# Down-projection prepared ahead, and four merge blocks beside the last head's close

## Chip, cores and metric

The kernel runs on one core of a Trainium2 chip. The metric is the device time of one execution in microseconds (us), the median of several runs. The core's engines are TensorE (PE in the profile, with its weight loads as PEld), VectorE (DVE), ScalarE (ACT), GpSimd (POOL) and SyncE (SP), whose queue here issues all DMAs. Each engine works through its own list in a fixed order.

## What is computed

One layer of a streaming encoder, for 1024 rows of a prompt and 8 x 16 rows of samples, 1152 rows of 1024 features in float32. Cut to what matters here:

```
# three mixers on slices of h @ w_in; B is a gated recurrence in 4 heads of 128
o_b = merge_heads(rms_norm_gated(o_b, hgrn_w, heads(bg, B_VAL_DIM)))
gates = sigmoid(gt.reshape(bsz, t, N_BRANCH, D_MODEL))
mix = gates[:, :, 0] * (o_a @ w_ba) + gates[:, :, 1] * (o_b @ w_bb) + gates[:, :, 2] * (o_c @ w_bc)
x = layer_norm(ALPHA * x + mix @ w_out, ln1_g, ln1_b)
up, new_ffn_conv = causal_dwconv(x @ w_up, buf_ffn, f_conv_w)     # 2 x 2816 columns
gate, val = split(up + f_conv_b, 2)
x = layer_norm(ALPHA * x + (silu(gate) * val) @ w_down, ln2_g, ln2_b)
```

## The kernel before

Rows of tokens are cut into three blocks of 384 (n = 0, 1, 2), features into tiles of 128. Each float32 operand is split in a high part and a rest, by a cast on ScalarE and a subtraction on VectorE, and a product is three matmuls: high by high, high by rest, rest by high. In the names, o, x1 and mix have parts with h and l, and whl, w8, wres and wd are weights with both parts.

A scheduler in the compiler orders each engine's list from the order of the program, the buffers and its own model of time. A pool gives each tag a ring of buffers; a new tile waits until the old one in its place is done with. `beside` puts a generator on a side list that `tick` advances between matmuls, so `yield 2` means "two ticks later". `drain` runs the side list out. `keep_in_program_order` holds an instruction at its place on its engine.

**The last head and the merge.** Heads of the mixers run as generators beside the projections' blocks. A head's last step, `finish_group` (L700), multiplies the head's output oT by its norm factor (L703; the factor comes from nine tiny VectorE operations named nwi, nwa, nwy), transposes it on PE (L148), multiplies it by the gate z2 (L709) and stores it to d_o. Then `load_o` (L1485) loads the four heads' outputs of a block of tokens and splits them into o (L1478, L1479); the last tile of four is called z. The merge multiplies o by the branch weights, 12 matmuls a block (24 blocks for branch 1: m = 0 to 7 for each n), and `branch_ev` (L1512) evicts each with a gate tile from d_g: one multiplication (L1517) and one addition into mix (L1518). Weights wb 0 to 3 lie in whl, 4 to 7 in wres (L1566, L1567). L1559 drains the side list, the last head among it, before the first block of branch 1. Then follow w_out (weights L1600) and the norm.

**Up-projection.** Column tiles come in 22 pairs of gate and value. From the third pair on, the token blocks 0 and 1 are done by a scheme of seven half-size products in place of eight, with sums of features (the four tiles ts) and of weights; block 2 is done plainly. `Pair.put` takes a product out of PSUM, `Pair.conv` does the convolution over three rows, which needs the two rows ahead of the block, and stores to d_gu.

**Down-projection.** It has 66 steps: for each half of the 22 feature tiles, for each token block n, for each tile k of the half. A step needs the weight rows wd[k] (loaded and split only for n = 0: L1957, L1958) and the features gd (two loads from d_gu, multiplied in L1962, split in L1965 and L1966). It makes 18 matmuls into six PSUM banks, for three row tiles by two halves of the columns; after eleven steps the six banks are added into yac (L2054). `residual` loads nine yac tiles and the norm's vectors gb (L1939) and turns them into the scaled residual (L1943, L1944). `prepare` (L2047) runs up to eight steps ahead. All of this is issued after the up-projection's last block and a drain.

Of the kernel before, what the change touches and what calls it, by code (L numbers as in the profile page):

```python
# [17 lines left out]
P = 128  # L18
# [53 lines left out]
def tile_encoder_step(ctx: ExitStack, tc: tile.TileContext, cst, x_prompt, x_sample, cache_k, cache_v, st_hgrn,  # L72
# [73 lines left out]
    def tr(out, in_):  # L146
        n = in_.shape[0]
        PE.transpose(out, in_, ident[:n, :n])  # L148
# [551 lines left out]

    def finish_group(oT, fac, wcol, z2, out):

        V.tensor_mul(u3(oT), u3(oT), bc(fac, 3))  # L703
# [688 lines left out]
    def b_finish(hd, n):  # L1392
        x, h = hd.g[n], hd.h

        so = small("rq2", [P, 3], 2)
        V.tensor_scalar(so, x.ss, 1.0 / P, 4 * RMS_EPS, ALU.mult, ALU.add)
        yield 1
        yield from finish_group(x.oT, rsqrt(cur[0], so, 3), vcol("hgw", 0), hd.z[n], d_o[1][h * P:(h + 1) * P, tok(n)])

# [33 lines left out]

    done = [0]

# [181 lines left out]

    oh, ol, _ = parts[1]
    mh = [[None] * NBLK for _ in range(KD)]
# [12 lines left out]
    for n in range(NBLK):  # L1632
        if n:
            beside(mix_split(n - 1))

        for i, m in enumerate((4, 5, 6, 7, 0, 1, 2, 3) if n == 2 else range(KD)):
            block(wb[m], oh, ol, n, branch_ev(1, m), kt=4)
            if n == 0 and i in (2, 5):
                load_in_turn(gb[:, i // 3], (ln_in_g, ln_in_b)[i // 3].partition_broadcast(P))
# [80 lines left out]
    class Pair:  # L1720
# [5 lines left out]
        def tail(self):  # L1726
            yield 5
# [94 lines left out]
    def x_sums():  # L1822
        for k in range(H):
            t = wfp_().bitcast(F32)
            t = t.rearrange("p a b c -> p (a b c)")[:, :4 * NW].rearrange("p (a w) -> p a w", w=NW)
            for a, (kk, n) in enumerate(((k, 0), (k, 1), (k + H, 0), (k + H, 1))):
                V.tensor_add(t[:, a], xh[kk][n].bitcast(F32), xl[kk][n].bitcast(F32))
                yield 1
# [5 lines left out]
            yield 1  # L1834
            hl = xs.tile([P, 2, 4, NW], F32R, name=f"ts{k}")
            S.copy(hl[:, 0], t)
# [42 lines left out]
    T1, T3, T4, T2 = ((lambda k, a=a: (ts[k][:, 0, a], ts[k][:, 1, a])) for a in range(4))  # L1879
    B11, B21, B22 = ((lambda k, k0=k0, n=n: (xh[k0 + k][n], xl[k0 + k][n])) for k0, n in ((0, 0), (H, 0), (H, 1)))  # L1880

# [9 lines left out]
    for i, pr in enumerate(rest):  # L1891
# [10 lines left out]
        p5 = product(pr.s12, 0, T1)  # L1902
        pr.put(0, 0, product(pr.a1, 1, B21), p1)
        pr.conv(0, 0)
        next(parts_[i + 1], None)
        V.tensor_add(u3, u2, product(pr.s34, 0, T3))
        V.tensor_add(u2, u2, p5)
        pr.put(1, 1, p5, u3)
        pr.put(0, 1, product(pr.s34, 1, B22), u2)
        pr.conv(0, 1)  # L1910
        gate_rest = lambda pr=pr: block(pr.a1, xh, xl, NBLK - 1, pr.ev(0))
        behind = lambda pr=pr: block(pr.a2, xh, xl, NBLK - 1, pr.ev(1))
        if i < len(rest) - 1:
            gate_rest()
            next(parts_[i + 1])
        pr.put(1, 0, product(pr.a2, 1, T4), u3)
        pr.conv(1, 0)
        pr.conv(1, 1)
    gate_rest()
    behind()  # L1920

    drain()
    xs_ctx.close()
    late.close()
    s0_ctx.close()
# [4 lines left out]
    yac = [yp.tile([P, D], F32, name=f"yac{j}") for j in range(NT)]  # L1930
    wd, gd = {}, {}
    late_w = lambda: dp.tile([P, 2, D], F32R, tag="wd", name=nm("wd"), bufs=12)

    def residual():
        gb = dp.tile([P, 2, D], F32, name="gb2")
        for i, src in enumerate((ln1_g[0], ln1_b[0])):
            load(gb[:, i], src.partition_broadcast(P))
        yield 6
        S.mul(gb, gb, ALPHA)  # L1939
        for j in range(NT):  # L1940
            load(yac[j], d_xn1[j * P:(j + 1) * P, :])
            yield 3
            V.tensor_mul(yac[j], yac[j], gb[:, 0])  # L1943
            V.tensor_add(yac[j], yac[j], gb[:, 1])  # L1944
            yield 3
        for t, src in enumerate((ln2_g, ln2_b)):
            load(gb[:, t], src[0].partition_broadcast(P))
        lnv.append(gb)

    lnv = []  # L1950

    def prep_step(half, n, k):
        if n == 0:
            raw = dp.tile([P, D], F32, tag="wdr", name=nm("wdr"), bufs=2)
            load(raw, w_down[0, k * P:(k + 1) * P, :])
            hl = wd[k] = late_w()
            S.copy(hl[:, 0], raw)  # L1957
            V.tensor_sub(hl[:, 1], raw, hl[:, 0].bitcast(F32))  # L1958
        raw = dp.tile([P, 2, NW], F32, tag="gr", name=nm("gr"), bufs=3)
        for half_ in range(2):  # L1960
            load(raw[:, half_], d_gu[half_][k][:, tok(n)])
        V.tensor_mul(raw[:, 0], raw[:, 0], raw[:, 1])  # L1962
        raw = raw[:, 0]
        g = gd[k, n] = dp.tile([P, 2, NW], F32R, tag="gd", name=nm("gd"), bufs=13)
        S.copy(g[:, 0], raw)  # L1965
        V.tensor_sub(g[:, 1], raw, g[:, 0].bitcast(F32))  # L1966

    def terms(ps, k, n, i, cs, first, stop):
        g, sl = gd[k, n], slice(i * P, (i + 1) * P)
        mm(ps, g[:, 0, sl], wd[k][:, 0, cs], start=first, stop=False)  # L1970
        mm(ps, g[:, 1, sl], wd[k][:, 0, cs], start=False, stop=False)
        mm(ps, g[:, 0, sl], wd[k][:, 1, cs], start=False, stop=stop)

# [28 lines left out]
    def last_ln(j):  # L2002
        y = yac[j]
        g2, b2 = lnv[0][:, 0], lnv[0][:, 1]
        if j == NT - 1:
# [19 lines left out]
        V.tensor_scalar(s[:, 2:3], s[:, 0:1], s[:, 1:2], -1.0 / D, ALU.add, ALU.mult)  # L2025
        squares = dp.tile([P, D], F32, tag="wdr", name=nm("wdr"), bufs=2)
        S.activation(squares, y, AF.Square, bias=s[:, 2:3], accum_out=s[:, 3:4])
# [14 lines left out]
    cols = [slice(hf * 512, (hf + 1) * 512) for hf in range(2)]  # L2042
    rows_of = [range(0, NFF // 2), range(NFF // 2, NFF)]
    steps = [(half, n, k) for half in range(2) for n in range(NBLK) for k in rows_of[half]]
    ahead = [0]

    def prepare(upto):  # L2047
# [4 lines left out]
    def put_sum(half, j, hf, ps):  # L2052
        if half == 0 or j == NT - 1:
            V.tensor_add(yac[j][:, cols[hf]], yac[j][:, cols[hf]], ps)  # L2054
# [65 lines left out]
```

## Time and profile before

| | us |
|---|---|
| median of 3 runs | 2266.27 (2265.26 to 2268.82) |
| the profiled execution | 2266.73 |
| its span in the trace | 2264.9 |
| TensorE busy | 2178.8 (96%) |
| VectorE busy | 1530.2 (68%) |
| ScalarE busy | 982.7 (43%) |

A row of a timeline has the start in us, the duration (of all merged instructions together), the engine, the line, the operation, output and inputs, the count, and in brackets how long the engine was idle before and what ended that. Matmuls overlap, so the rate is read from the starts of rows. The trace's clock of TensorE over the whole run was 0.985 of full.

### The profile page before, as it was taken

The page shows a single profiled execution, that of the slowest core. Times are in us where ns is not written, and L with a number is a line of the kernel's source. Part 1 is how long each engine was busy: PE and PEld are TensorE (multiplying, and loading weights), DVE is VectorE, ACT ScalarE, POOL GpSimd, SP SyncE. Part 2 cuts the span into 40 slices and gives each one's busy share as a digit, 9 for nine tenths or more (in the row PEclk, how much of TensorE's full clock was granted, in tenths as well). Part 3 has the DMA queues.
Part 4 walks back from the last instruction along what each step waited for, and adds up shares of the span by engine and source line. Part 5 has one row for each costly group of instructions (what it writes and reads, how often), then busy time and mean ns, then how long its engine had stood idle before and what let it go on. Part 6 is the DMA issues. An engine that isn't in the chain of part 4 may idle for free.

```text
span 2264.9 us, 35159 instructions
## 1 busy us (share of the span) xinstructions
PE 2178.8 (96%) x12759; PEld 2030.1 (90%) x12759; DVE 1530.2 (68%) x4246; ACT 982.7 (43%) x2309; POOL 1.3 (0%) x9
## 2 busy tenths in 40 slices
PE   7999999999999999999999899999999999689998
PEld 7998889999999999999989888899999999567886
DVE  7367556666765657767878786877777777674444
ACT  4356434344345346355433333544545445231234
POOL 0000000000000000000000000000000000000000
PEclk9999999999999999999999999999999999899999
DMA  5121231222222221312354541232323232674421
GB/s 139 44 76 56 86 102 48 74 73 65 69 78 57 76 60 52 94 42 64 119 157 137 164 151 75 70 102 94 102 97 108 92 97 76 224 233 128 155 98 56
DMA packets 261373, 220.30 MB, mean 97 GB/s; under 512 B 38810, under 2 KB 250688, under 8 KB 261184
## 3 DMA queue, kind: packets, MB, share of 16 engines
q1 hardware_dynamic: 261200, 218.06, 31.1%
q8 instruction: 100, 1.64, 0.3%
q14 instruction: 73, 0.60, 0.1%
HBM read 152.86 MB, written 66.06 MB: 97 GB/s over the span
## 4 chain that ended last, share of the span: by engine, by line
PE 85%; DVE 5%; DMA 5%; ACT 3%; issue 1%; SPq 1%; DVEq 0%; ACTq 0%
PE psg L108 72%; PE psp L108 5%; PE psch L108 4%; DMA gr<-d_gu 2%; PE psp L148 2%; PE psch L148 1%; PE psms L108 1%; PE psms L148 1%; DMA xp<-d_o 1%; SPq L111 1%; DVE gr L1962 0%; DVE yac L1944 0%; DVE gd L1966 0%; ACT L1223 0%; DVE yac L1943 0%
## 5 line engine op out<-in xcount | busy, mean ns | idle before, releaser
L108 PE MATMUL psg<-hh,whl 128*128 128x384 f32 x2976 | 809.0, 344 | 0.8 <-ACT qf L436 0.7
L108 PEld LDWEIGHTS psg<-hh,whl 128*128 128x128 f32 x2976 | 535.6, 188 | 15.4 <-issue 8.6
L108 PE MATMUL psg<-hl,whl 128*128 128x384 f32 x1488 | 508.5, 342 | 0.0
L108 PE MATMUL psg<-wd,gd 128*128 128x512 f32 x1188 | 277.0, 396 | 30.9 <-ACT gd L1965 11.2
L108 PEld LDWEIGHTS psg<-wd,gd 128*128 128x128 f32 x1188 | 227.1, 192 | 80.6 <-ACT gd L1965 11.4
L108 PEld LDWEIGHTS psg<-hl,whl 128*128 128x128 f32 x1488 | 280.1, 188 | 4.3 <-issue 2.6
L108 PE MATMUL psg<-x1h,w 128*128 128x384 f32 x672 | 182.0, 340 | 0.0
L108 PE MATMUL psg<-x1h,whl 128*128 128x384 f32 x640 | 172.7, 339 | 2.8 <-ACT whl L212 1.2
L108 PE MATMUL psg<-o,whl 128*128 128x384 f32 x720 | 142.8, 349 | 6.6 <-ACT o L1478 2.6
L108 PEld LDWEIGHTS psg<-o,whl 128*128 128x128 f32 x720 | 127.3, 194 | 9.8 <-ACT o L1478 3.2
L108 PEld LDWEIGHTS psg<-x1h,w 128*128 128x128 f32 x672 | 122.9, 188 | 1.0
L108 PEld LDWEIGHTS psg<-x1h,whl 128*128 128x128 f32 x640 | 116.9, 189 | 4.9 <-ACT whl L212 1.9
L108 PE MATMUL psg<-x1l,w 128*128 128x384 f32 x336 | 113.5, 338 | 0.0
L213 DVE TENSOR_TENSOR whl<-wraw,whl 128x1024 fp32r<-128x1024 f32 (+1 forms) x82 | 91.5, 1117 | 31.9 <-ACT whl L212 30.8
L108 PE MATMUL psg<-x1l,whl 128*128 128x384 f32 x320 | 108.2, 338 | 0.0
L108 PE MATMUL psg<-ts,w 128*128 128x384 f32 x576 | 105.8, 334 | 0.0
L108 PEld LDWEIGHTS psg<-ts,w 128*128 128x128 f32 x576 | 100.6, 188 | 0.0
L1962 DVE TENSOR_TENSOR gr<-gr 128x384 f32<-128x384 f32 x66 | 36.7, 557 | 92.7 <-DMA gr<-d_gu 92.2
L212 ACT CAST whl<-wraw 128x1024 fp32r<-128x1024 f32 (+1 forms) x82 | 79.0, 964 | 36.8 <-PE psg L108 34.4
L108 PE MATMUL psg<-wres,mixh 128*128 128x512 f32 x288 | 92.5, 395 | 0.0
L1965 ACT CAST gd<-gr 128x384 fp32r<-128x384 f32 x66 | 33.8, 512 | 129.5 <-PE psg L108 78.3
L1445 ACT ACTIVATE ga<-psg 128x384 f32<-128x384 f32 x72 | 35.4, 491 | 97.6 <-PE psg L108 80.0
(505 smaller groups left out, 3829.1 us busy)
## 6 DMA issues: line engine op xcount, KB each, us to landing
wraw<-in_w_in_dram SPq DMA_DIRECT2D x58, 512.0 KB
gr<-d_gu SPq DMA_DIRECT2D x132, 192.0 KB
d_g<-ga SPq DMA_DIRECT2D x72, 192.0 KB
wraw<-in_w_up_dram SPq DMA_DIRECT2D x24, 512.0 KB
wdr<-in_w_down_dram SPq DMA_DIRECT2D x22, 512.0 KB
wr<-in_w_up_dram SPq DMA_DIRECT2D x20, 512.0 KB
acc<-d_g SPq DMA_DIRECT2D x48, 192.0 KB
d_gu<-ga SPq DMA_DIRECT2D x44, 192.0 KB
```

What stands on the lines that cost most here:

```text
L108: PE.matmul(out, lhsT, rhs, start=start, stop=stop)
L111: nc.sync.dma_start(out=out, in_=in_)
L148: PE.transpose(out, in_, ident[:n, :n])
L212: S.copy(hl[:, 0, :kt, :cols], raw[:, :kt, :cols])
L213: V.tensor_sub(hl[:, 1, :kt, :cols], raw[:, :kt, :cols], hl[:, 0, :kt, :cols].bitcast(F32))
L1445: S.activation(g, ps, AF.Tanh, scale=0.5)
L1962: V.tensor_mul(raw[:, 0], raw[:, 0], raw[:, 1])
L1965: S.copy(g[:, 0], raw)
```

## The change

At the end of the mixers, the program no longer drains before branch 1: it ticks only until the last head is about to finish (`ended`), issues the weights and the first four blocks of the merge (m = 0 to 3, n = 0), and then drains. The last head's `finish_group` waits ten ticks, and its first transpose is held in its place.

In the up-projection, the roles of token blocks 0 and 1 in the scheme of seven are exchanged, so that block 0 of the value and of the gate are taken out and convolved together; an output chain (`tail`) waits ten ticks, not five. The tiles ts come from a ring of four.

The down-projection's first two weights, in the buffers wraw and whl, and the features of its first four steps, in one tile g4 in the ring of ts, are prepared ahead of the up-projection's last two blocks (`ending`). Steps 2 and 3 have their raw weights loaded there too. yac lies in the other three tiles of that ring, three rows of tokens in each, and `residual` is run once for each token block. Features have two buffers of raw data and twelve split ones (three and thirteen before), weights twelve in all as before, two of them whl. `put_sum` gets a higher priority with the scheduler.

```diff
-    def finish_group(oT, fac, wcol, z2, out):
+    def finish_group(oT, fac, wcol, z2, out, behind=False):
         V.tensor_mul(u3(oT), u3(oT), bc(fac, 3))
-        yield 2
+        yield 10 if behind else 2
         ps = psum("ms")
         for i in range(3):
-            tr(ps[:, i * P:(i + 1) * P], oT[:, i * P:(i + 1) * P])
+            t = PE.transpose(ps[:, i * P:(i + 1) * P], oT[:, i * P:(i + 1) * P], ident)
+            if behind and i == 0:
+                tc.keep_in_program_order(t)
...
-    drain()
+    while not ended[0]:
+        tick()
...
     whl_pair(2)
+
+    oh, ol, _ = parts[1]
+    for m in range(4):
+        block(wb[m], oh, ol, 0, branch_ev(1, m), kt=4)
+    drain()
...
-    for m in range(3):
+    for m in range(4, 7):
         gate_ahead[1, m, 0] = load_gate(1, m, 0)
...
+            if n == 0 and i < 4:
+                continue
             block(wb[m], oh, ol, n, branch_ev(1, m), kt=4)
...
-        pr.put(0, 0, product(pr.a1, 1, B21), p1)
-        pr.conv(0, 0)
+        pr.put(0, 1, product(pr.a1, 1, B21), p1)
...
-        pr.put(1, 1, p5, u3)
-        pr.put(0, 1, product(pr.s34, 1, B22), u2)
+        pr.put(1, 0, p5, u3)
+        pr.conv(1, 0)
+        pr.put(0, 0, product(pr.s34, 1, B22), u2)
+        pr.conv(0, 0)
         pr.conv(0, 1)
...
+    def prep_weights(k):
+        raw, hl = raw_w(), two_w()
+        load(raw, w_down[0, k * P:(k + 1) * P, :])
+        S.copy(hl[:, 0], raw)
+        V.tensor_sub(hl[:, 1], raw, hl[:, 0].bitcast(F32))
+        wd[k] = hl
+
+    def prep_features(n, k, raw, gh, gl):
+        for half in range(2):
+            load(raw[half], d_gu[half][k][:, tok(n)])
+        V.tensor_mul(raw[0], raw[0], raw[1])
+        S.copy(gh, raw[0])
+        V.tensor_sub(gl, raw[0], gh.bitcast(F32))
+        gd[k, n] = gh, gl
+
+    EARLY = 4
+    g4 = quarter_of_xs("g4")
+    for s in range(EARLY):
+        if s < 2:
+            prep_weights(s)
+        prep_features(0, s, [s0_piece("gr", F32) for _ in range(2)], g4[:, 0, s], g4[:, 1, s])
+    ahead[0] = EARLY
+    ending()
     drain()
...
+    for k in range(2, EARLY):
+        prep_weights(k)
...
     def put_sum(half, j, hf, ps):
-        if half == 0 or j == NT - 1:
-            V.tensor_add(yac[j][:, cols[hf]], yac[j][:, cols[hf]], ps)
-        else:
-            add_and_sum(j, hf, cols[hf], ps)
+        with tc.high_priority(60):
...
-            if (half, n) == (0, 0):
-                prepare(3)
-                beside(residual())
+            if half == 0:
+                beside(residual(n), 12 if n == 0 else 1)
...
-                    prepare(min(at + 8, 3 + 2 * at))
+                    prepare(at + 8 if at > 1 else at + 6 + at)
```

How this moves instructions on the engines is shown at three places. First PE, at the last head's close: psms is the transposed output of the last head, psg with whl or wres the blocks of branch 1. Before:

```order
L108 MATMUL psg_14526<-o_13770,whl_14385 128x384
L108 MATMUL psg_14526<-o_13769,whl_14385 128x384
L148 MATMUL psms_14348<-call,oT_14211 128x128 x3
L108 MATMUL psg_14601<-o_14463,whl_14439 128x384
L108 MATMUL psg_14601<-o_14464,whl_14439 128x384
```

and of the change:

```order
L108 MATMUL psg_14526<-o_13769,whl_14378 128x384
L108 MATMUL psg_14572<-o_14463,whl_14439 128x384
...
L108 MATMUL psg_14623<-o_14481,whl_14567 128x384
L707 MATMUL psms_14422<-call,oT_14211 128x128 x3
L108 MATMUL psg_14669<-o_14463,wres_14658 128x384
L108 MATMUL psg_14669<-o_14464,wres_14658 128x384
L108 MATMUL psg_14685<-o_14463,wres_14658 128x384
```

The transposes moved behind the four blocks (psg_14572 to psg_14623, 48 matmuls), and what comes next on PE needs wres.

On ScalarE, what casts wres stands behind the cast of the last head's z tile, in both programs. Of the change:

```order
L1572 CAST whl_14567<-wraw_14568 128x1024
L1483 CAST o_14557<-v_14555 128x384
L1483 CAST o_14563<-z_14561 128x384
L1572 CAST wres_14658<-wraw_14659 128x1024
L1572 CAST wres_14663<-wraw_14664 128x1024
```

Here nothing moved; PE's rows around it did.

Second VectorE at the same place, one piece of the difference: the rows with acc are evictions of the four blocks (psg_14572 and on), those with mix their additions, and oT is what the transposes wait for.

```order
+L1522 SCALAR_TENSOR_TENSOR acc_14619<-acc_14619,psg_14606 128x384
+L1523 TENSOR_TENSOR mix_12568<-mix_12568,acc_14602 128x384
 L327 SCALAR_TENSOR_TENSOR nwy_14318<-nwa_14315,nwi_14312 128x3
+L1523 TENSOR_TENSOR mix_12571<-mix_12571,acc_14619 128x384
 L324 TENSOR_TENSOR nwa_14320<-nwy_14318 128x3
+L1522 SCALAR_TENSOR_TENSOR acc_14636<-acc_14636,psg_14623 128x384
 L325 SCALAR_TENSOR_TENSOR nwa_14320<-nwa_14320,rq_3024_14297 128x3
+L1523 TENSOR_TENSOR mix_12574<-mix_12574,acc_14636 128x384
 L327 SCALAR_TENSOR_TENSOR nwy_14323<-nwa_14320,nwy_14318 128x3
```

All four blocks' evictions now stand inside the chain of small operations that leads to oT; before, they stood behind it.

Third the DMA queue of SP, where the up-projection ends. d_gu<-gv are its last feature stores, wdr and wraw raw down-projection weights, gr features, yac residual rows. Before:

```order
L111 DMA yac_21665<-d_xn_118 128x1024
L111 DMA d_gu_21_16097<-gv_21591 128x384
...
L111 DMA d_gu_21_16119<-gv_21631 128x384
L111 DMA wdr_21668<-in_w_down_dram 128x1024
L111 DMA gr_21673<-d_gu_0_16076 128x384
L111 DMA gr_21673<-d_gu_0_16098 128x384
```

and of the change:

```order
L111 DMA wraw_21694<-in_w_down_dram 128x1024
L111 DMA d_gu_20_16118<-gv_21423 128x384
L111 DMA wraw_21699<-in_w_down_dram 128x1024
...
L111 DMA d_gu_21_16119<-va_21492 128x384
...
L111 DMA d_gu_21_16119<-gv_21670 128x384
L111 DMA out_dram<-r_4256_21676 16x128
L111 DMA gr_21718<-d_gu_4_16080 128x384
L111 DMA gr_21718<-d_gu_4_16102 128x384
L111 DMA gr_21730<-d_gu_5_16081 128x384
```

The weights of steps 2 and 3 are now loaded about one pair earlier, those of steps 0 and 1 earlier still; behind the last store stand the features of step 4, and no residual rows stand ahead of it.

More of the change, by code (lines that the diff above doesn't have):

```diff
@@ L1396, in b_finish @@
         V.tensor_scalar(so, x.ss, 1.0 / P, 4 * RMS_EPS, ALU.mult, ALU.add)
+        last = (h, n) == (3, NBLK - 1)
         yield 1
-        yield from finish_group(x.oT, rsqrt(cur[0], so, 3), vcol("hgw", 0), hd.z[n], d_o[1][h * P:(h + 1) * P, tok(n)])
+        ended[0] = last
+        yield from finish_group(x.oT, rsqrt(cur[0], so, 3), vcol("hgw", 0), hd.z[n], d_o[1][h * P:(h + 1) * P, tok(n)],
+                                last)
     heads = []
@@ L1432, in b_group @@
         done[0] += 1
-    done = [0]
+    done, ended = [0], [False]
     GT = 4872
@@ L1616, in rows_h @@
         V.tensor_add(t, t, gb[:, 1])
-    oh, ol, _ = parts[1]
     mh = [[None] * NBLK for _ in range(KD)]
@@ L1636, in tile_encoder_step @@
         for i, m in enumerate((4, 5, 6, 7, 0, 1, 2, 3) if n == 2 else range(KD)):
+            if n == 0 and i < 4:
+                continue
             block(wb[m], oh, ol, n, branch_ev(1, m), kt=4)
-            if n == 0 and i in (2, 5):
-                load_in_turn(gb[:, i // 3], (ln_in_g, ln_in_b)[i // 3].partition_broadcast(P))
+            if n == 0 and i in (4, 6):
+                load_in_turn(gb[:, i // 2 - 2], (ln_in_g, ln_in_b)[i // 2 - 2].partition_broadcast(P))
             if n == 1 and i == 3:
@@ L1726, in tail @@
         def tail(self):
-            yield 5
+            yield 10
             ps1 = psum("ms")
@@ L1811, in tile_encoder_step @@
     xs = xs_ctx.enter_context(tc.tile_pool(name="xs", bufs=1, side="right", reuse_waits="tile"))
+    quarter_of_xs = lambda name: xs.tile([P, 2, 4, NW], F32R, tag="ts", name=nm(name), bufs=4)
     H = KD // 2
@@ L1825, in x_sums @@
             t = t.rearrange("p a b c -> p (a b c)")[:, :4 * NW].rearrange("p (a w) -> p a w", w=NW)
-            for a, (kk, n) in enumerate(((k, 0), (k, 1), (k + H, 0), (k + H, 1))):
+            for a, (kk, n) in enumerate(((k, 1), (k, 0), (k + H, 1), (k + H, 0))):
                 V.tensor_add(t[:, a], xh[kk][n].bitcast(F32), xl[kk][n].bitcast(F32))
@@ L1834, in x_sums @@
             yield 1
-            hl = xs.tile([P, 2, 4, NW], F32R, name=f"ts{k}")
+            hl = quarter_of_xs("ts")
             S.copy(hl[:, 0], t)
@@ L1879, in tile_encoder_step @@
     T1, T3, T4, T2 = ((lambda k, a=a: (ts[k][:, 0, a], ts[k][:, 1, a])) for a in range(4))
-    B11, B21, B22 = ((lambda k, k0=k0, n=n: (xh[k0 + k][n], xl[k0 + k][n])) for k0, n in ((0, 0), (H, 0), (H, 1)))
+    B11, B21, B22 = ((lambda k, k0=k0, n=n: (xh[k0 + k][n], xl[k0 + k][n])) for k0, n in ((0, 1), (H, 1), (H, 0)))
     beside(x_sums())
@@ L1914, in tile_encoder_step, with ending @@
             gate_rest()
-            next(parts_[i + 1])
-        pr.put(1, 0, product(pr.a2, 1, T4), u3)
-        pr.conv(1, 0)
+            next(parts_[i + 1], None)
+        pr.put(1, 1, product(pr.a2, 1, T4), u3)
         pr.conv(1, 1)
-    gate_rest()
-    behind()
+    def ending():
+        gate_rest()
+        behind()
+    raw_w = lambda: wp.tile([P, D], F32, tag="wraw", name=nm("wraw"), bufs=2)
+    two_w = turn(*2 * [lambda: wp.tile([P, 2, D], F32R, tag="whl", name=nm("whl"), bufs=2)],
+                 *10 * [lambda: dp.tile([P, 2, D], F32R, tag="wd", name=nm("wd"), bufs=10)])
@@ new lines, in tile_encoder_step @@
+    wd, gd = {}, {}
+    rows_of = [range(0, NFF // 2), range(NFF // 2, NFF)]
+    steps = [(half, n, k) for half in range(2) for n in range(NBLK) for k in rows_of[half]]
+    ahead = [0]
+    def prep_weights(k):
[11 more added lines that the diff above has]
+        gd[k, n] = gh, gl
@@ L1930, in tile_encoder_step @@
[L1930 to L1942, printed above, removed]
+    yac = []
@@ new lines, in tile_encoder_step, with residual @@
+    for n in range(NBLK):
+        y3 = quarter_of_xs("yac").bitcast(F32).rearrange("p a b c -> p (a b c)")
+        yac += [y3[:, i * D:(i + 1) * D] for i in range(3)]
+    for k in range(2, EARLY):
+        prep_weights(k)
+    gb = dp.tile([P, 2, D], F32, name="gb2")
+    def residual(n):
+        if n == 0:
+            for i, src in enumerate((ln1_g[0], ln1_b[0])):
+                load_in_turn(gb[:, i], src.partition_broadcast(P))
+            S.mul(gb, gb, ALPHA)
+            yield 2
+        for j in range(3 * n, 3 * n + 3):
+            load_in_turn(yac[j], d_xn1[j * P:(j + 1) * P, :])
+            yield 4
@@ L1943, in residual @@
             V.tensor_mul(yac[j], yac[j], gb[:, 0])
             V.tensor_add(yac[j], yac[j], gb[:, 1])
[L1945 to L1950, printed above, removed]
-    def prep_step(half, n, k):
[L1953 to L1966, printed above, removed]
+            yield 1
@@ L1968, in terms @@
+        if n == NBLK - 1:
+            for t, src in enumerate((ln2_g, ln2_b)):
+                load_in_turn(gb[:, t], src[0].partition_broadcast(P))
+    def prep_step(half, n, k):
+        if n == 0 and k not in wd:
+            prep_weights(k)
+        raw = dp.tile([P, 2, NW], F32, tag="gr", name=nm("gr"), bufs=2)
+        g = dp.tile([P, 2, NW], F32R, tag="gd", name=nm("gd"), bufs=12)
+        prep_features(n, k, [raw[:, i] for i in range(2)], g[:, 0], g[:, 1])
     def terms(ps, k, n, i, cs, first, stop):
-        g, sl = gd[k, n], slice(i * P, (i + 1) * P)
@@ L1970, in terms @@
-        mm(ps, g[:, 0, sl], wd[k][:, 0, cs], start=first, stop=False)
-        mm(ps, g[:, 1, sl], wd[k][:, 0, cs], start=False, stop=False)
-        mm(ps, g[:, 0, sl], wd[k][:, 1, cs], start=False, stop=stop)
+        gh, gl = (g[:, i * P:(i + 1) * P] for g in gd[k, n])
+        mm(ps, gh, wd[k][:, 0, cs], start=first, stop=False)
+        mm(ps, gl, wd[k][:, 0, cs], start=False, stop=False)
+        mm(ps, gh, wd[k][:, 1, cs], start=False, stop=stop)
     row_sums = {}
@@ L2003, in last_ln @@
         y = yac[j]
-        g2, b2 = lnv[0][:, 0], lnv[0][:, 1]
+        g2, b2 = gb[:, 0], gb[:, 1]
         if j == NT - 1:
@@ L2025, in last_ln @@
         V.tensor_scalar(s[:, 2:3], s[:, 0:1], s[:, 1:2], -1.0 / D, ALU.add, ALU.mult)
-        squares = dp.tile([P, D], F32, tag="wdr", name=nm("wdr"), bufs=2)
+        squares = raw_w()
         S.activation(squares, y, AF.Square, bias=s[:, 2:3], accum_out=s[:, 3:4])
@@ L2042, in tile_encoder_step @@
     cols = [slice(hf * 512, (hf + 1) * 512) for hf in range(2)]
-    rows_of = [range(0, NFF // 2), range(NFF // 2, NFF)]
-    steps = [(half, n, k) for half in range(2) for n in range(NBLK) for k in rows_of[half]]
-    ahead = [0]
     def prepare(upto):
@@ L2052, in put_sum @@
     def put_sum(half, j, hf, ps):
-        if half == 0 or j == NT - 1:
-            V.tensor_add(yac[j][:, cols[hf]], yac[j][:, cols[hf]], ps)
-        else:
-            add_and_sum(j, hf, cols[hf], ps)
+        with tc.high_priority(60):
+            if half == 0 or j == NT - 1:
+                V.tensor_add(yac[j][:, cols[hf]], yac[j][:, cols[hf]], ps)
+            else:
+                add_and_sum(j, hf, cols[hf], ps)
         if half and hf:
@@ L2087, in tile_encoder_step @@
     drain()
+    late.close()
     xs_ctx.close()
-    late.close()
+    wp_ctx.close()
     banks["ctx"].close()
```

3 lines of the change are left out of this document (removed).

## The prediction

> **What bounds the kernel now.** I read the page first, then the waits of PE, then the two places that they point to in the timelines of PE, VectorE, ScalarE and the DMA queue.
>
> ```profile
> PE   7999999999999999999999899999999999689998
> ```
>
> PE's busy share is 9 tenths or more in nearly every slice, so only a stretch in which PE stands still can give time back. A slice is 56.6 us. After the start, the low digits are the 8 around 1250 us and the pair 6, 8 from 1925 to 2038 us: the end of the last head, and the start of the down-projection. The change touches just these two. PE's own rows there (the bracket holds the idle time before a row and what ended it):
>
> ```profile
> 1945.80 0.29 PE L148 MATMUL psms<-call,l 128*36 128x128 f32 x1 [0.87 <-ACT l L1753]
> 1957.29 12.54 PE L108 MATMUL psg<-wd,gd 128*128 128x512 f32 x48 [11.20 <-ACT gd L1965]
> 1977.59 4.45 PE L108 MATMUL psg<-wd,gd 128*128 128x512 f32 x12 [7.76 <-DVE wd L1958]
> 1990.35 35.91 PE L108 MATMUL psg<-wd,gd 128*128 128x512 f32 x149 [8.31 <-DVE gd L1966]
> 2028.01 32.25 PE L108 MATMUL psg<-wd,gd 128*128 128x512 f32 x141 [1.75 <-DVE yac L2054]
> ...
> 2074.85 179.17 PE L108 MATMUL psg<-wd,gd 128*128 128x512 f32 x782 [1.90 <-DVE yac L2054]
> ```
>
> The down-projection runs from 1945.80 to the last eviction at 2254.06 (chain row below), 308.3 us. Its undisturbed stretch makes 782 matmuls in 179.17 us, 0.2291 us each.
>
> ```profile
> 2254.06 0.70 DVE yac L2054
> ...
> L108 PE MATMUL psg<-wd,gd 128*128 128x512 f32 x1188 | 277.0, 396 | 30.9 <-ACT gd L1965 11.2
> ```
>
> All 1188 at that pace are 272.2 us, so the stage holds 36 us that are not work: three long waits (27.3), two for evictions (3.7), and the rest at a halved clock after the waits. What ends them:
>
> ```profile
> 1949.71 0.34 SPq L111 DMA_DIRECT2D d_gu<-gv  x1
> 1950.53 0.36 SPq L111 DMA_DIRECT2D wdr<-in_w_down_dram  x1
> ...
> 1954.56 1.04 ACT L1957 CAST wd<-wdr 128x1024 fp32r<-128x1024 f32 x1 [6.33 <-DMA wdr<-in_w_down_dram]
> ...
> 1956.61 1.22 DVE L1958 TENSOR_TENSOR wd<-wdr,wd 128x1024 fp32r<-128x1024 f32 x1
> ...
> 1965.62 10.31 DVE L1943 TENSOR_TENSOR yac<-yac,gb 128x1024 f32<-128x1024 f32 x9 [3.19 <-ACT gb L1939]
> ...
> 1982.93 6.89 DVE L1944 TENSOR_TENSOR yac<-yac,gb 128x1024 f32<-128x1024 f32 x6
> ```
>
> The first weights are loaded only after the last feature store (1949.71); that is the 11.2. The other two waits stand behind VectorE, which does all nine residual rows in blocks of 10.3 and 6.9 us ahead of the weights and features of steps 2 and 3.
>
> **The down-projection, part by part.** Four feature steps and two weight steps are now ready before the up-projection's last blocks, and the raw weights of steps 2 and 3 are loaded (order rows of SP above). PE can then go on behind the transpose at 1945.80. A step is 18 matmuls, 4.12 us. Step 2 is due at 1946.1 + 8.2 = 1954.3. Its VectorE part stands behind the last feature row, which ended at 1949.7, and two subtractions of 1.22 us (L1958) end at 1952.2. Step 4 is due at 1962.6. Its loads can start about 1950.5, as before; the first step before took 6.8 us from the load (1950.53) to PE (1957.29), and one subtraction more makes about 1959. So no wait there, by some 3 us.
>
> After that supply must outrun PE:
>
> ```profile
> DMA packets 5434, 9.91 MB, mean 283 GB/s; under 512 B 610, under 2 KB 4465, under 8 KB 5431
> ...
> gr<-d_gu SPq DMA_DIRECT2D x28, 192.0 KB
> wdr<-in_w_down_dram SPq DMA_DIRECT2D x7, 512.0 KB
> ```
>
> This is the DMA view of 1995 to 2030 us: 14 feature steps and 7 weights in 35 us. A fresh step (two feature loads, one weight) is 0.92 MB, or 3.2 us at that rate, under PE's 4.12. The nine residual rows now come three per token block, spread between steps, and are not needed before the first eviction about 1990. I cost them at nothing; VectorE is their cover, and if a block of three fell ahead of a step it would cost up to 10.31 / 3 = 3.4 us.
>
> Evictions get priority. They cost 3.7 us before; between 0 and 3.7 I take 1.9. The stage is then 0.3 + 272.2 + 1.9 = 274.4 us: **33.9 us less**.
>
> The early work itself is two casts and two subtractions of weights, and four multiplications, casts and subtractions of features. What such operations take, and how VectorE stands in the up-projection:
>
> ```profile
> L1962 DVE TENSOR_TENSOR gr<-gr x37: 547/558/560, 1956.1 to 2077.2; 128x384 f32<-128x384 f32 x37
> L1965 ACT CAST gd<-gr x35: 505/514/516, 1956.7 to 2070.8; 128x384 fp32r<-128x384 f32 x35
> L1966 DVE TENSOR_TENSOR gd<-gr,gd x35: 547/551/560, 1957.7 to 2078.3; 128x384 fp32r<-128x384 f32 x35
> ```
>
> ```profile
> 1930.22 0.56 DVE L1744 TENSOR_TENSOR xp<-psg,p 128x384 f32<-128x384 f32 x1 [3.11 <-PE psg L108]
> ...
> 1937.85 1.22 DVE L1770 SCALAR_TENSOR_TENSOR va<-xp,fvec,va 128x384 f32<-128x384 f32 x2
> ```
>
> That is 2 x 1.22 + 4 x (0.56 + 0.55) = 6.9 us of VectorE, beside PE in the up-projection, where VectorE waits for PE (3.11). Without that cover it would cost at most those 6.9 us. On the DMA queue eight feature loads and four weight loads move ahead among the up-projection's; at 0.36 us an issue (1950.53) that is 4.3 us of a queue that nobody waits for there, so nothing. In the same loop three convolutions now come in a row, about six VectorE passes of 0.62 us (L1770). Seven PSUM banks, 12 matmuls or some 2 us each, stand in front of PE, so I take 0, with 0 to 4 us (0.2 us in each of 20 pairs) for the range. A gain is excluded, since PE did not wait there.
>
> **The end of the last head.** PE, VectorE, DMA queue and ScalarE:
>
> ```profile
> 1245.14 2.16 PE L108 MATMUL psg<-o,whl 128*128 128x384 f32 x11
> 1254.43 0.88 PE L148 MATMUL psms<-call,oT 128*128 128x128 f32 x3 [7.13 <-DVE oT L703]
> 1254.96 11.10 PE L108 MATMUL psg<-o,whl 128*128 128x384 f32 x48
> 1265.90 8.48 PE L108 MATMUL psg<-o,wres 128*128 128x384 f32 x48
> ...
> 1302.02 2.38 PE L108 MATMUL psg<-o,whl 128*128 128x384 f32 x12 [0.59 <-DVE x L1517]
> 1306.16 4.43 PE L108 MATMUL psg<-o,whl 128*128 128x384 f32 x24 [1.76 <-DVE x L1517]
> ```
>
> ```profile
> 1251.04 0.55 DVE L1479 TENSOR_TENSOR o<-v,o 128x384 fp32r<-128x384 f32 x1
> ...
> 1253.53 0.16 DVE L327 SCALAR_TENSOR_TENSOR nwy<-nwa,nwy 128x3 f32<-128x3 f32 x1
> 1253.73 0.56 DVE L703 TENSOR_TENSOR oT<-oT,nwy 128x384 f32<-128x384 f32 x1
> ...
> 1258.29 0.32 SPq L111 DMA_DIRECT2D z<-d_o  x1
> ...
> 1260.59 0.51 ACT L1478 CAST o<-z 128x384 fp32r<-128x384 f32 x1 [11.80 <-DMA z<-d_o]
> 1261.01 2.00 ACT L1566 CAST wres<-wraw 128x1024 fp32r<-128x1024 f32 x2
> ```
>
> On the DMA queue the four blocks' gate loads now stand ahead of two weight loads, which leave when VectorE frees their buffers, as before.
>
> The four blocks that move (the 48 matmuls of 1254.96) fill the gap of 7.13 us: at full clock 8.48 us, from 1247.3 to 1255.7. But VectorE's order now has their eight evictions inside the chain that makes oT. Identical up to 1251.5, it waits for the fourth block (1255.7), then has an eviction and an addition of 0.55, five small passes 0.2 apart and oT's 0.56: the transposes start about 1258.4, not 1254.43. Behind them comes the chain of store, load and ScalarE's cast of z, 6.16 us before (1254.43 to 1260.59), some 5.8 with the transposes at full clock: 1264.2. The casts of the next weights, wres, stand **behind that cast** in ScalarE's order, before and after. Before, the four blocks covered this wait. Now nothing does: wres is cast by 1265.7 (0.42 + 1.05 us later), and PE starts its block there, against 1265.90. The lead of 8 us is given back.
>
> What is late next is the clock:
>
> ```profile
> 1250.00:1252.00 2.00, 0.00 (x0) 0.00 (x0) 2.00 (x4) 0.00 (x0) 0.00 (x0) 0.56 0.00 0
> ...
> 1260.00:1262.00 2.00, 2.00 (x12) 2.00 (x11) 0.56 (x1) 1.41 (x3) 0.00 (x0) 0.88 0.93 278
> ...
> 1960.00:1962.00 2.00, 2.00 (x10) 1.64 (x9) 1.89 (x4) 0.75 (x2) 0.00 (x0) 0.95 0.90 367
> ```
>
> (The last three numbers are granted clock, DMA share and GB/s.) PE stopped at 1247.3 and its clock fell to half about 3 us later; it came back 6 us after PE's restart at 1254.43, and 3 us after that at 1957.29. The new wait from 1258.9 to 1265.7 is 6.8 us, so the same happens, now behind 1265.7: a loss of half of 3 to 6 us, of which I take 2.3. The shorter one ahead of the transposes (2.7 us) should not trip it. Against that, a later PE may find the evictions of 1302 and 1306 done (0.59 + 1.76); between 0 and 2.4 I take 1.2. The merge is **1.1 us more**, from -2.4 to +5 (no absorption, a longer half clock, and 2 us more should the fourth gate's load be late).
>
> [...]
>
> **Sum.** The profiled execution took 2266.73 us, 0.46 over the median. 2266.73 - 33.9 + 1.1 = 2233.9, on the median 2233.5.
>
> **Rivals.**
> - The merge pays too: wres and its subtraction are ready in time, so that the 7.13 us and the half clock (3.1) go. For it: the weights themselves land early. Against: the order of ScalarE. That is 10.2 instead of -1.1: 2222.
> - One landing shows: step 2 or 4 comes late because its loads or tiles are released late, and PE waits once for a load (6.8 us, as above) and at half clock (3.1): 2243. For it: the new tiles lie where the up-projection's lay. Against: 3 us of slack.
> - The change does not do what it says: the early features come into a tile that the last product still reads, and PE again waits 11.2 us, with 3.1 at half clock. The residual's two waits still go: 2248. Against: that product (the row below) was past its first tile ten microseconds ahead.
>
> ```profile
> 1934.23 2.24 PE L108 MATMUL psg<-ts,w 128*128 128x384 f32 x12
> ```
>
> - Slower: features now turn in two buffers, not three. From load to release must then take under two steps, 8.2 us. If it took 10, each of the 66 steps would take 5.0: 330 us, so 2266.3 + 21.7 + 1.1 = 2289; it decides from 9.3 us, where the loss eats the whole gain. Against it, the longest feature load on the chain of waits:
>
> ```profile
> 1992.31 6.86 DMA gr<-d_gu
> ```
>
> With the three passes that is 6.86 + 0.56 + 0.51 + 0.55 = 8.5 us, at worst and for one load.
>
> **Chances.** Forecast 0.70, merge pays 0.07, a landing shows 0.14, not what it says 0.04, slower by the buffers 0.05. The forecast's own bounds are 2228 (no eviction waits, merge -2.4) to 2243 (evictions 3.7, merge +5, convolutions +4). The range, 2227 to 2246, adds the late landing and leaves out some 0.15. A change under 0.2% (4.5 us) could hardly be told from none; only a mix of the last two cases ends there. Faster 0.94, same 0.02, slower 0.04.
>
> **What would show it.** Right: no PE wait over 1 us from 1945 to 1990; residual rows of VectorE in threes; two PE gaps at the last head, one of 2 to 3 us ahead of the transposes and one of 6 to 7 behind them that ScalarE's cast of wres ends; half clock once there and not in the down-projection. Wrong: a PE wait for a cast or subtraction at steps 0 to 6, PE waits inside the up-projection's pairs, feature steps further apart than 4.2 us, or a merge without the second gap.

## The result, and the profile after

| | before | after |
|---|---|---|
| median | 2266.38 us (4 runs) | 2244.9 us (4 runs, 2242.7 to 2246.05) |
| ratio to before | | 0.9903, 95% interval 0.9885 to 0.992 |
| profiled execution | 2266.73 us, span 2264.9 | 2245.49 us, span 2243.7 |

The kernel is 21.5 us faster. The forecast was 2233.5 us, so 11.4 us of the forecast gain are missing.

PE's slices of the changed kernel, on its page; the pair 6, 8 at the start of the down-projection is gone:

```profile
PE   7999989999999999999999899999999999999998
```

PE's rows at the two places (start, duration, what, and in brackets the idle time before and what ended it):

```profile
1255.95 0.52 PE L707 MATMUL psms<-call,oT 128*128 128x128 f32 x3 [2.58 <-DVE oT L703]
1262.85 10.78 PE L108 MATMUL psg<-o,wres 128*128 128x384 f32 x48 [6.38 <-ACT wres L1572]
...
1307.77 0.39 PE L108 MATMUL psg<-wres,mixh 128*128 128x512 f32 x1
...
1946.64 0.29 PE L148 MATMUL psms<-call,l 128*36 128x128 f32 x1 [0.87 <-ACT l L1765]
1946.68 8.68 PE L108 MATMUL psg<-whl,g 128*128 128x512 f32 x36
1955.20 8.56 PE L108 MATMUL psg<-wd,g 128*128 128x512 f32 x36
1963.60 29.56 PE L108 MATMUL psg<-wd,gd 128*128 128x512 f32 x126
1993.00 2.73 PE L108 MATMUL psg<-whl,gd 128*128 128x512 f32 x11
1997.36 6.08 PE L108 MATMUL psg<-whl,gd 128*128 128x512 f32 x25 [1.62 <-DVE yac L2089]
2003.28 37.96 PE L108 MATMUL psg<-wd,gd 128*128 128x512 f32 x162
2041.08 2.96 PE L108 MATMUL psg<-whl,gd 128*128 128x512 f32 x12
2048.99 7.41 PE L108 MATMUL psg<-whl,gd 128*128 128x512 f32 x24 [4.96 <-DVE yac L2089]
```

From 1946.64 to the first eviction (1997) PE never waits: the three long waits of the kernel before (27.3 us) are gone, as forecast. But one new thing is seen in the counts: 36 matmuls from 1955.20 to 1963.60 are 233 ns each, where the kernel before took 227. The rows of 80 undisturbed microseconds, before (first) and after (second), say it at a glance; the columns are busy time and count of PE, weight loads, VectorE, ScalarE and GpSimd, then granted clock, DMA share, GB/s:

```profile
2100.00:2180.00 80.00, 80.00 (x355) 66.24 (x354) 40.26 (x89) 27.56 (x64) 0.00 (x0) 1.00 0.40 129
```

```profile
2100.00:2180.00 80.00, 80.00 (x345) 64.45 (x344) 33.91 (x85) 24.07 (x59) 0.00 (x0) 1.00 0.36 114
```

PE is busy throughout, at full clock, in both, yet makes 345 matmuls instead of 355. The starts of consecutive matmuls are 226.7 ns apart before and 233.3 after, over the whole down-projection.

Where the time went, stage by stage, from the starts of the rows of each profiled execution (the merge is counted from the last matmul of psch<-bv,kT to the first of w_out, the up-projection from there to the transpose at 1946.64, the down-projection from there to its last matmul):

| us | ahead of the merge | merge | up-projection (its matmuls at half clock, 320 ns) | down-projection |
|---|---|---|---|---|
| before | 1245.1 | 65.3 | 635.4 (7) | 307.8 |
| after | 1242.9 | 64.9 | 638.9 (24) | 285.8 |

The first column is scatter: nothing in it is changed, and in the profiled executions of this study it lies between 1242.1 and 1246.3. The last column holds the whole gain, 22.1 us of the 33.9 forecast.

### The profile page after: what moved, and what is told of

It is laid out like the page before. It is cut to its first block, busy times and chain, and to the rows that moved or that the text cites. A ratio compares the mean times of both kernels' runs of the same rounds, so it can differ in the third digit from the quotient of the medians.

```text
span 2243.7 us, 35146 instructions
## 1 busy us (share of the span) xinstructions
PE 2181.9 (97%) x12759; PEld 2028.6 (90%) x12759; DVE 1532.1 (68%) x4246; ACT 978.0 (44%) x2309; POOL 1.3 (0%) x9
## 4 chain that ended last, share of the span: by engine, by line
PE 86%; DVE 5%; DMA 4%; ACT 4%; issue 1%; SPq 0%; DVEq 0%; ACTq 0%
PE psg L108 73%; PE psp L108 5%; PE psch L108 4%; PE psp L148 2%; DMA gr<-d_gu 1%; PE psms L108 1%; PE psch L148 1%; DMA wraw<-in_w_out_dram 1%; DMA xp<-d_o 0%; SPq L111 0%; DMA yac<-d_xn 0%; ACT L1225 0%; DVE gr L1957 0%; PE psms L148 0%; PE psms L707 0%
## 5 line engine op out<-in xcount | busy, mean ns | idle before, releaser
L108 PE MATMUL psg<-wd,gd 128*128 128x512 f32 x936 | 220.8, 395 | 0.0
L108 PEld LDWEIGHTS psg<-wd,gd 128*128 128x128 f32 x936 | 175.9, 188 | 42.5
L213 DVE TENSOR_TENSOR whl<-wraw,whl 128x1024 fp32r<-128x1024 f32 (+1 forms) x82 | 91.5, 1117 | 32.0 <-ACT whl L212 30.9
L1779 ACT ACTIVATE va<-xp,fvec 128x384 f32<-128x384 f32 (+1 forms) x66 | 47.1, 716 | 84.2 <-DVE xp L1775 83.9
```

The costliest lines, as they stand in the source:

```text
L108: PE.matmul(out, lhsT, rhs, start=start, stop=stop)
L213: V.tensor_sub(hl[:, 1, :kt, :cols], raw[:, :kt, :cols], hl[:, 0, :kt, :cols].bitcast(F32))
L1779: S.activation(acc[:, :w], xp[:, 2:2 + w], AF.Identity, scale=fvec[:, 2, ct:ct + 1], bias=fvec[:, 3, ct:ct + 1])
```

## The experiments

All ratios are to runs of the kernel before on the same chip, so experiments are compared with each other by their ratios. The times of one kernel spread over 1 to 8 us, so counts and waits in the trace decide where terms are small.

**Addresses of the operands.** What differs between the 233.3 ns matmuls and the others? Not the instruction. The compiled programs give the start addresses (bytes in each partition) of the streamed weights (wd, whl) and the stationary features (gd). The runs e1, e2 and e8 follow below:

```
          wd        gd        gd - wd modulo 256
before    0x7380    0x21780   0
after     0xb360    0x22b80   32
e1        0x7380    0x217a0   32
e2        0xb360    0x22b60   0
e8        0x7380    0x21880   0
```

The early features (g) of the changed kernel lie 128 off and run at 233.3 too (the rows from 1955.20 above). The 384-column matmuls of the kernel before, sorted by the same difference, take 174.1 ns at 0 (some 5900 of them) and 176.0 at 128 (some 1400). So the theory was put to three shifts.

```diff
             hl = wd[k] = late_w()
+            if k == 0:
+                dp.tile([P, 8], F32, name="shift")
```

> The kernel before with one change: an unused tile of 32 bytes per partition between the weights' tiles (wd) and the features' (gd), so that all features of the down-projection lie 32 bytes further. No instruction changes. Theory: a matmul takes longer when the addresses of its two operands differ modulo 256 bytes. In the kernel before they are equal (pace 226.7 ns), in the changed kernel they differ by 32 (233.3 ns). Then the pace here becomes 233.3 ns and the time grows by 1188 x 6.6 ns = 7.8 us, to about 2274. Rival: the slower pace comes from what else the change moved (weights in another pool, more traffic of the other engines): pace 226.7 and time 2266 as before.

Measured (e1): 2271.71 us against 2265.4, ratio 1.0026 (1.0016 to 1.0036). The same 80 us:

```profile
2100.00:2180.00 80.00, 80.00 (x344) 64.43 (x343) 38.97 (x84) 24.75 (x56) 0.00 (x0) 1.00 0.40 126
```

Exactly the changed kernel's pace, from 32 unused bytes in the kernel before. The time grows by 6.3 us; the 7.8 us are partly met by shorter waits (the five in the down-projection sum to 28.8 us instead of 30.9).

```diff
-    three_halves = dp.tile([P, 1], F32, name="three_halves")
-    V.memset(three_halves, 1.5)
...
+    prepare(6)
+    three_halves = dp.tile([P, 1], F32, name="three_halves")
+    V.memset(three_halves, 1.5)
     at = 0
```

> The changed kernel with the small tile three_halves allocated behind the features' tiles instead of ahead of them, so that gd lies 32 bytes lower and agrees with wd modulo 256 bytes; its one memset moves behind the first prepared steps. Theory of the addresses: the 1116 matmuls that read gd go at 226.7 ns instead of 233.3, 7.4 us less: about 2237.5. The two eviction waits (6.6 us) stay. Rival (the pace comes from the new pools or traffic): 2245 as the changed kernel.

Measured (e2): 2240.67 us, ratio 0.9896 (0.9881 to 0.9911). This interval overlaps that of the changed kernel, so here the pace decides, not the time. The same 80 us of this kernel:

```profile
2100.00:2180.00 80.00, 80.00 (x355) 66.26 (x354) 33.89 (x88) 24.00 (x59) 0.00 (x0) 1.00 0.36 114
```

The pace is back at 226.7 ns, and the down-projection takes 281.1 us instead of 285.8. Of the 7.4 us, 2 go to the eviction waits, which grow from 6.6 to 8.6, probably because a faster PE reaches them sooner.

```diff
             hl = wd[k] = late_w()
+            if k == 0:
+                dp.tile([P, 64], F32, name="shift")
```

> The kernel before with an unused tile of 256 bytes between weights and features, in place of the 32 bytes of the first run. Theory of the addresses modulo 256: pace 226.7 ns and 2265 to 2266, as before. Rival (any shift of the features slows the matmuls): 233.3 ns and 2272.

Measured (e8): 2266.5 us, ratio 1.0003 (0.9993 to 1.0012), and the count is that of before. The shift of 256 bytes costs nothing (355 matmuls in 80 us); the one of 32 in e1 cost 6.6 ns a matmul (344). By the pace the rivals fall in all three runs. The 80 us of e8:

```profile
2100.00:2180.00 80.00, 80.00 (x355) 66.24 (x354) 40.51 (x92) 27.89 (x63) 0.00 (x0) 1.00 0.41 131
```

**The two parts of the change apart.** First the merge's hunks alone on the kernel before, then the others alone.

> The kernel before with the merge's part of the change alone (four blocks ahead of the last head's close, the gate loads and the rows of gbin that go with it). Theory, from the changed kernel's profile (the stretch from the last block of the first branch to the first block of w_out is 63.2 us after and 63.1 before): no change, 2264 to 2269, with two PE waits of about 2.6 and 6.4 us in place of one of 7.1. Rival: this part costs the 11 us that the forecast missed: about 2277.

Measured (e3): 2267.98 us, ratio 1.0011 (1.0003 to 1.002); the merge takes 64.8 us, with PE waits of 2.6 and 6.4 us. (The 63.2 of the expectation was read from a row 0.5 us behind the first of w_out.) The part brings no gain; by the interval it loses 0.7 to 4.5 us, though the merge itself is 0.5 us shorter in the trace than before.

> The kernel before with the other part of the change alone (the up-projection's order and the early work of the down-projection). Theory: it carries the whole gain, 2243 to 2247, with a matmul pace of 233.3 ns in the down-projection and two eviction waits of about 6.6 us together. Rival (the merge's part costs 11 us): 2234.

Measured (e4): 2245.45 us, ratio 0.9916 (0.9903 to 0.9928); pace 233.3 ns, eviction waits 6.2 us, down-projection 286.4. The whole gain is here, and the missing 11 us are too.

**The eviction waits.** Why does PE wait 4.96 us ahead of 2048.99, although the evictions have priority? VectorE and the DMA queue of the changed kernel there:

```profile
2038.92 0.56 DVE L1957 TENSOR_TENSOR gr<-gr 128x384 f32<-128x384 f32 x1 [1.11 <-DMA gr<-d_gu]
...
2041.36 1.22 DVE L1992 TENSOR_TENSOR yac<-yac,gb 128x1024 f32<-128x1024 f32 x1 [0.67 <-DMA yac<-d_xn]
...
2044.58 1.22 DVE L1992 TENSOR_TENSOR yac<-yac,gb 128x1024 f32<-128x1024 f32 x1
...
2048.26 1.28 DVE L2089 TENSOR_TENSOR yac<-yac,psg 128x512 f32<-128x512 f32 x2
```

```profile
2016.70 20.05 SPq L111 DMA_DIRECT2D gr<-d_gu  x16
```

PE is done with the banks by 2044, but VectorE's order has two rows of the next block and several feature steps ahead of the eviction, and works them off until 2048.26. It is late with the features, which come no faster than 8 steps (16 loads) in 20 us, 2.5 us each.

```diff
-                beside(residual(n), 12 if n == 0 else 1)
+                beside(residual(n), 12)
```

> The changed kernel with the residual rows of blocks 1 and 2 starting 12 ticks into their block, as those of block 0 do, instead of 1. On VectorE two of block 2's rows (2.45 us each) stood ahead of block 1's evictions; now they stand among or behind them. Theory: the PE wait of 5.0 us at 2049 goes, and the half clock after it (10 matmuls at 427 ns, 1.9 us); of the 6.6 us of eviction waits some 2 stay: 2245 - 6 = 2239. The matmul pace stays 233.3 ns. Rival: the wait comes from somewhere else (the rows' loads, the feature steps on VectorE) and another wait takes its place: 2245.

Measured (e5): 2244.24 us, ratio 0.9902 (0.9885 to 0.9918). The waits fall from 6.6 to 4.0 us and the down-projection from 285.8 to 283.5, too little to see in the time. The rows are only a part. VectorE now has feature steps alone ahead of the eviction, each waiting for its load:

```profile
2043.12 0.56 DVE L1957 TENSOR_TENSOR gr<-gr 128x384 f32<-128x384 f32 x1 [0.21 <-DMA gr<-d_gu]
2044.33 0.56 DVE L1959 TENSOR_TENSOR gd<-gr,gd 128x384 fp32r<-128x384 f32 x1 [0.65 <-ACT gd L1958]
2045.87 0.56 DVE L1957 TENSOR_TENSOR gr<-gr 128x384 f32<-128x384 f32 x1 [0.98 <-DMA gr<-d_gu]
2046.35 0.68 DVE L2089 TENSOR_TENSOR yac<-yac,psg 128x512 f32<-128x512 f32 x1
```

```diff
-        raw = dp.tile([P, 2, NW], F32, tag="gr", name=nm("gr"), bufs=2)
-        g = dp.tile([P, 2, NW], F32R, tag="gd", name=nm("gd"), bufs=12)
+        raw = dp.tile([P, 2, NW], F32, tag="gr", name=nm("gr"), bufs=3)
+        g = dp.tile([P, 2, NW], F32R, tag="gd", name=nm("gd"), bufs=11)
```

> The changed kernel with the residual rows 12 ticks into their block, as in the run before (which still had an eviction wait of 3.8 us), and with three buffers for the raw features (gr) in place of two, eleven for the split ones (gd) in place of twelve. Addresses stay 32 bytes apart: pace 233.3 ns. Theory: VectorE's order has ten feature steps of the next block ahead of block 1's evictions, and with two raw buffers these go no faster than the loads, one in 2.4 us, so VectorE is still at them when PE ends the block; with three they go faster and the wait of 3.8 us becomes under 1.5: 2244 - 4 = 2240, with half clock gone too. Rival: the loads themselves, not the buffers, set the 2.4 us, and the wait stays: 2244.

Measured (e9): 2241.96 us, ratio 0.9889 (0.9874 to 0.9903). The waits are 2.8 us and the down-projection 280.4, at the same pace. The step from e5 to e9 also moved rows on VectorE, so buffers and order are not told apart; together the two edits take 5.4 us off the stage, in one profiled execution of each kernel.

**z behind wres.** Of the last head's rows, ScalarE holds the next:

```profile
1261.34 0.51 ACT L1483 CAST o<-z 128x384 fp32r<-128x384 f32 x1 [14.79 <-DMA z<-d_o]
1261.76 1.99 ACT L1572 CAST wres<-wraw 128x1024 fp32r<-128x1024 f32 x2
```

```diff
+                if (br, n, k) == (1, NBLK - 1, 3):
+                    continue
                 raw = tmp[0]()
...
         pair(m, mp.tile([P, 2, 4, 2 * P], F32R, tag="wres", name=nm("wres"), bufs=8))
+    raw = mr.tile([P, NW], F32, name="zraw")
+    load(raw, d_o[1][3 * P:4 * P, tok(NBLK - 1)])
+    oh[3][NBLK - 1], ol[3][NBLK - 1] = split(raw, "o")
```

> The changed kernel with the last head's z (load, cast, subtraction) issued behind the casts and subtractions of the two wres weights of blocks 4 to 7 instead of ahead of them. Theory: ScalarE's cast of z waits 14.8 us for the store and load of o, and wres stands behind it; with the order turned, wres is ready when PE has done the transposes: the wait of 6.4 us goes, and most of the half clock after it (2.3 us): 2245 - 8 = 2237. Rival: the time is given back later (z comes 2 to 3 us later, the gates of blocks 4 to 7 or the evictions become the wait): 2243 to 2245.

Measured (e6): 2243.85 us, ratio 0.99 (0.9883 to 0.9916). The waits of PE in the merge, then the row of its last 38 us:

```profile
PE psg L108 <- DVE x L1524: 4.2, 4, 1.8
PE psms L707 <- DVE oT L703: 2.6, 1, 2.6
PE psg L108 <- DVE wres L1575: 0.4, 1, 0.4
```

```profile
1268.00:1306.00 38.00, 34.33 (x191) 33.04 (x192) 34.31 (x59) 18.33 (x25) 0.00 (x0) 1.00 0.65 213
```

The wait of 6.4 us is down to 0.4, so its cause is shown: it was the order of ScalarE. But the waits for evictions behind it grow from 0.7 to 4.2 us, with VectorE busy 34.3 of 38 us. The merge becomes 61.4 us, 3.5 less instead of 8. In the later runs that have this edit too (e7, e10, e11, e12) it takes 61.8 to 64.6 us, so the gain is 0.3 to 3.5 us.

**All together.** e7 has the three edits (e2, e5, e6), e10 the three raw buffers besides, e11 and e12 vary what stands ahead of the evictions.

> The changed kernel with all three edits: features 32 bytes lower (addresses equal modulo 256 bytes), residual rows 12 ticks into their block, z behind wres. If the three terms add up: 2245 - 7 - 6 - 8 = 2224, pace 226.7 ns. If the rivals hold for the two orders, 2237.

Measured (e7): 2235.24 us, ratio 0.9863 (0.9847 to 0.9879): the lowest median of all runs, and faster than both kernels. The terms do not add up to 2224, and the rivals' 2237 is nearer. The pace is 226.7 ns again, but the down-projection takes 278.5 us, with 6.2 us of eviction waits left, and the merge 64.5: its eviction waits are 5.4 us, and about ten matmuls behind the last of them run at half clock (24 matmuls take 6.01 us there, 4.46 in e6).

> The kernel with all three edits (addresses, residual rows, z behind wres) and also three raw feature buffers. If the buffers are the cause of the eviction wait of 4.5 us that it still had: 2235 - 5 = 2230, pace 226.7 ns. Rival: 2235.

Measured (e10): 2237.4 us, ratio 0.987 (0.9853 to 0.9886), not to be told from e7. The eviction waits are 4.9 us. The features now come in PE's own step, 4.0 us apart, so VectorE is no longer behind with them; what stands ahead of the late eviction is a pair of residual rows and one feature step. The features:

```profile
2032.46 0.56 DVE L1963 TENSOR_TENSOR gr<-gr 128x384 f32<-128x384 f32 x1 [2.95 <-DMA gr<-d_gu]
...
2036.46 0.56 DVE L1963 TENSOR_TENSOR gr<-gr 128x384 f32<-128x384 f32 x1 [2.97 <-DMA gr<-d_gu]
```

> The kernel with all three edits and the features prepared 6 steps ahead of PE in place of 8, two raw buffers as in the changed kernel. Fewer feature steps then stand ahead of the evictions on VectorE. Theory (the evictions wait behind feature steps that were ordered far ahead): the wait of 4.5 us falls below 2: 2235 - 4 = 2231. Rival: the eviction wait moves to the residual rows or PE waits for features: 2235 or more.

Measured (e11): 2238.01 us, ratio 0.9874 (0.9859 to 0.9889); eviction waits 7.6 us. The rival came: VectorE's order then has a pair of the third block's residual rows ahead of the first eviction, which e7 has behind it. What the shorter look-ahead would be worth with the rows in their old place stays open.

> The kernel with all three edits and three raw feature buffers, and with the residual rows of blocks 1 and 2 starting 16 ticks into their block (block 0: 12). In VectorE's order no residual row then stands ahead of block 1's evictions. Theory: the eviction waits that were left (4.9 us, of which 2.9 behind a row pair and a feature step) fall under 2, the half clock after them goes, and the down-projection takes 270 to 273 us in place of 277.8: about 2232. Rival: the third block's rows now come late and its evictions wait instead: 2237.

Measured (e12): 2240.38 us, ratio 0.9877 (0.9856 to 0.9898), with a down-projection of 280.7 us. The second block's wait falls from 2.9 to 1.7 us, but the third's evictions wait 6.5. PE's waits in its down-projection, then VectorE ahead of the third block's evictions:

```profile
PE psg L108 <- DVE yac L2093: 8.1, 2, 6.5
```

```profile
2062.00 1.22 DVE L1999 TENSOR_TENSOR yac<-yac,gb 128x1024 f32<-128x1024 f32 x1
...
2086.77 1.22 DVE L1957 TENSOR_TENSOR wd<-wraw,wd 128x1024 fp32r<-128x1024 f32 x1
2089.87 0.56 DVE L1963 TENSOR_TENSOR gr<-gr 128x384 f32<-128x384 f32 x1 [1.88 <-DMA gr<-d_gu]
2090.35 0.55 DVE L1965 TENSOR_TENSOR gd<-gr,gd 128x384 fp32r<-128x384 f32 x1
2090.82 1.28 DVE L2093 TENSOR_TENSOR yac<-yac,psg 128x512 f32<-128x512 f32 x2
```

The time is the rival's, or worse, but not for its reason. The third block's last residual row (L1999) is done at 2063.2, long before PE stops at 2085. Its evictions stand behind feature and weight steps of the second half, the last of which waits for its load.

## Why the prediction was right, and which term was mis-sized

**The down-projection** was right in kind: early features and weights came in time, no wait ended by a load, cast or subtraction is left. Its sum, 0.3 + 272.2 + 1.9 = 274.4 us from the transpose to the last eviction, was short by 11.8. The changed kernel takes 286.2, from the transpose quoted above to its last eviction:

```profile
2232.83 0.69 DVE L2089 TENSOR_TENSOR yac<-yac,psg 128x512 f32<-128x512 f32 x1 [3.87 <-PE psg L108]
```

- *The pace*, "all 1188 at that pace are 272.2 us". The step taken for granted was that a matmul of the same shape takes the same time after its operands have moved. Here it did not (226.7 ns before, 233.3 after): 1188 x 0.2333 = 277.2, 5.0 more. The term was doubly off. The row it came from (782 in 179.17), called undisturbed, held seven matmuls at half clock (427 ns, from 2076.4); the undisturbed 226.7 ns would have given 269.3. At this pace the price of the addresses is thus 7.8 us; e1 and e2 show the pace, and the median of e1 shows 6.3 us of it.
- *The evictions*, "between 0 and 3.7 I take 1.9". They cost 6.6, 4.7 more, and 1.4 at half clock behind the longer one (seven matmuls at 427 ns). The priority did not put them first: in VectorE's order features and rows stood ahead of the eviction (the rows to 2048.26 above), and these ran late. The forecast spoke of a block of rows ahead of a step (3.4 us), but looked for the harm in the feature steps, not in the evictions. e5 and e9 show this place. The sign "half clock once there and not in the down-projection" therefore failed.

5.0 + 4.7 + 1.4 are 11.1 of the 11.8.

**The merge** was right in each step: transposes behind a wait of 2.58 us (2 to 3 forecast), then 6.38 (6 to 7) ended by ScalarE's cast of wres, thirteen matmuls at half clock (320 ns) behind it, 1.9 us (2.3), and later eviction waits 1.6 us shorter (1.2). Net +1.1 was forecast; the profile says -0.4, e3 alone +2.6 in the median. The rival "the merge pays too" was rightly small: even without the wait (e6) VectorE's evictions give more than half of it back.

**The up-projection** was put at 0, with 0 to 4 for the convolutions. It took 3.5 more in the profiled execution, yet not for the convolutions: the added half clock lies near 1452 and 1480, ahead of 1483.2, where the first product with ts starts, and behind waits that the kernel before has too. With the same order the stage takes 635.3 in e2 and 635.5 in e7, as before. But in seven of the ten profiled executions with the new order it takes 637.5 to 638.9, and in only one of four with the old (e3, 637.4; the others 635.3 or 635.4). Whether the change makes this half clock more likely stays open. The granted clock there, the first number of the last three, before (first) and after (second):

```profile
1450.00:1460.00 10.00, 8.39 (x44) 7.55 (x45) 9.65 (x16) 4.37 (x13) 0.00 (x0) 1.00 0.40 111
```

```profile
1450.00:1460.00 10.00, 8.62 (x41) 8.20 (x39) 9.08 (x16) 3.69 (x9) 0.00 (x0) 0.83 0.70 202
```

**The rivals.** No landing showed, and the change does what it says. The two feature buffers did not slow the steps to 5.0 us, since the loads came in 2.5; but they probably keep VectorE from catching up ahead of a block's end (e10 with three buffers is no longer behind with features). The time lay inside the range partly by luck: what filled the gap was not what the range had been widened for, which was a late landing, a longer merge and the convolutions.

## What to carry to other kernels

When tiles move to another pool, compare the start-to-start time of undisturbed matmuls before and after, and the addresses of the two operands; in e1 an unused tile of 32 bytes ahead of one of them cost 3% of each matmul (226.7 to 233.3 ns). When waits for loads are taken out of a stage, look next at what the static order of the evicting engine has ahead of the evictions, since late rows there became a PE wait here (4.96 us at 2048.99). And when a wait is removed by order alone, ask whether the engine behind it has idle time to take up the lead: in the merge VectorE had little, 3.7 of 38 us.

## What the runs showed of the hardware

- The time of a matmul went with where its operands lie. With 512 fp32r columns it is 226.7 ns where the addresses of the streamed and the stationary operand differ by a multiple of 256 bytes (before, e2, e8), and 233.3 ns at 32 bytes (after, e1) and at 128 (the early g of the changed kernel); with 384 columns, in the kernel before, 174.1 and 176.0 at 0 and 128 (in different loops, so less cleanly). In e1, e2 and e8 the pace follows this difference alone: the changed kernel has gd where the kernel before has it modulo 256 and is slow, and e2 has both operands elsewhere and is fast. Why it is so, and what other differences cost, was not tried.
- Half clock also came without a long wait. In the stretch shown above PE's longest idle time is 1.22 us before and 1.33 us after, and the granted clock is 1.00 in one execution and 0.83 in the other. Over the up-projection 7 matmuls before and 24 after run at 320 ns in place of 174, so 17 more, 2.5 of the 3.5 us that the stage took longer. The same in the merge: behind an eviction wait of 1.8 us (1.79 in e7, 1.78 in e6), 24 matmuls take 6.01 us in e7, about ten of them at half clock, and 4.46 in e6, none at half clock. What sets the moment at which the clock falls, no run here shows.
